# A hybrid decoder block on one core: attention's values behind two mLSTM heads, mLSTM gate rows in one scan, merge gates' tanh in two groups

## The chip, the cores and the metric

The kernel runs on one core of one Trainium2 chip. The metric is the device time of one execution in microseconds (us). Three executions of the kernel before took 822.51, 823.02 and 824.59 us; the median is 823.02 us.

## What is computed

One decoder layer over 512 tokens of width 1024, in float32, with two mixers side by side, a gated merge of them, a ConvFFN and a per-layer embedding. What bears on the change:

```
h = rmsnorm(x); mq, mk, mv, mo, mi, mf, dq, dk, dv, gates = split(h @ w_in)
# branch A, mLSTM, 4 heads x 128: conv4 + SiLU on q and k, and per token and head
#   logf = log_sigmoid(f_pre);  b = cumsum(logf);  m = running maximum of (m + logf, i_pre)
#   weight of key s for query t (s <= t):  exp(b_t - b_s + i_s - m_t)
#   hm = (sum_s weight * (q_t . k_s) * v_s) / max(|sum_s weight * (q_t . k_s)|, exp(-m_t))
ya = (sigmoid(mo) * head_rmsnorm(hm)) @ w_br_m
# branch B, differential attention, 4 heads, queries and keys 2 x 64, values 128
a = softmax(q1 k1 + bias) - lam * softmax(q2 k2 + bias);  hd = a @ dv
yb = (head_rmsnorm(hd) * (1 - lam_init)) @ w_br_d
x = x + (sigmoid(g_a) * ya + sigmoid(g_b) * yb) @ w_out
x = x + ffn(rmsnorm(x));  x = x + ple(...);  out = rmsnorm(x)
```

## The kernel before

Tokens (512) lie along the free axis of most tiles, features on the 128 partitions. A float32 product is made of three single-pass products of split operands (`mm3`, L94): high by high, high by low, low by high, where `split` (L86) casts the high part on ScalarE (L88) and subtracts for the low part on VectorE (L89). `wload` (L100) loads a 512 KB chunk of a weight into one of two `raw` tiles by SyncE's queue and splits it into one of two `whi` and `wlo` tiles. So ScalarE's cast for a projection waits until TensorE has finished with the projection two before it. Such a projection (`proj`) is 24 matmuls of 128x512.

The string `ORDER` (L49) names the steps of the two mixers in the order in which the program records them: `mq0` and `mk0` are projections with convolution and SiLU (`conv_silu`, L215), `if0` the gate rows (`gates`, L314), `ct0` their transposition (L355), `m0` the scores, weights and sums of mLSTM head 0 (`mlstm`, L413), `M0` and `N0` its end and norm, `dv0` the 96 matmuls of the attention's values (`vproj`, L286), `a0` and `A0` an attention head and its norm, `ga0` and `gb0` merge gates (`gate`, L531). What is not in the table (eight of the sixteen merge gates) is made in the merge loop (L580). The framework's scheduler then fixes one order for each engine, by its own estimate of times; weight loads are recorded with a priority ahead of their place. The engines run in that order, each waiting for semaphores at the head of its queue, so a waiting instruction holds up all behind it on that engine.

`gates` makes a 4-row (one per head) log forget gate `lf` and input gate `gi`, and the running maximum `m` by one scan (L341). Then for each of four key blocks j of 128 it scans `lf` again from the block's start (L346), subtracts for the key's column factor (L347), subtracts `m` for the query rows (L348) and writes the rows to `rd` in DRAM (L349). A last row, min(-m, 41), goes there too (L351, L352). `mlstm` loads each block's row as `rb`, broadcast over the partitions (L419), and exponentiates it with the transposed column as bias (L420). `mlstm_end` loads the last row as `em` (L445) and exponentiates it (L446).

In the merge loop a sigmoid is 0.5 + 0.5 tanh(x/2). The tanh of four gates of each pass is recorded behind the last softmax (`issue_after`, L583 to L585). Head 3's norm (`attention_end`, L504) takes a reciprocal root by Ln, Exp and Square (`rsqrt_of`, L152), which need another function table than tanh does.

Of the kernel before, what the change touches and what calls it, by code (L numbers as in the profile page):

```python
# [30 lines left out]
EM_MAX = 41.0  # L31
# [6 lines left out]
C_B = 256  # L38
# [3 lines left out]
ROW_OFF = [0, 512, 896, 1152, 1280]  # L42
# [4 lines left out]


ORDER = """  # L49
if0 mq0 mk0 mq1 mk1 ct0 m0 m1 mk3 mq2 dk0 M0 M1 mk2 bias0 m2 mq3 M2 m3 dq0 dv0 M3 a0 dk1 dq1  # L50
A0 a1 N0 A1 dk2 dq2 N1 ga3 dq3 a2 N2 A2 ga0 ga2 gb1 dk3 N3 a3 gb3 gb2 gb0 ga1 A3
"""


# [1 line left out]
def trunk_kernel(ctx, tc, xT, pT, par, biasT, lamv, w_if, w_in, w_v, w_br, w_out, w_up,  # L56
                 w_down, w_gate, w_ple, gfin, out):
    nc = tc.nc
# [59 lines left out]
    prm = cp.tile([P, NPAR], F32, name="prm")  # L118
# [25 lines left out]
    def sumsq_add(acc, src, first):  # L144
        if first:
            nc.scalar.activation(acc, src, AF.Square)
        else:
            q = tt("hn", "sq")
            nc.scalar.activation(q, src, AF.Square)
            nc.vector.tensor_add(acc, acc, q)  # L150

    def rsqrt_of(r, v, a, before=None, ss=None, n=P):  # L152

        if before is not None:
            with tc.issue_after(before.ins):
                nc.scalar.preload_act_table_set("natural_log_exp_and_others")
        if ss is None:
            nc.scalar.activation(r, v, AF.Ln, scale=2.0 ** -LN_SHIFT)
        else:
            nc.scalar.activation(r, ss, AF.Ln, scale=2.0 ** -LN_SHIFT / n, bias=epsb)  # L160
        nc.scalar.activation(r, r, AF.Exp, scale=-0.5, bias=lnb)
        nc.scalar.activation(a, r, AF.Square)
        nc.vector.scalar_tensor_tensor(a, v, -0.5, a, op0=ALU.mult, op1=ALU.mult)
        nc.vector.scalar_tensor_tensor(r, a, 1.5, r, op0=ALU.add, op1=ALU.mult)

# [17 lines left out]
    h = []  # L183
# [11 lines left out]
    ident = cp.tile([P, P], F32, name="ident")  # L195
# [3 lines left out]
    rB = None  # L199
# [86 lines left out]
    def vproj(i, name, first=None):  # L286
# [24 lines left out]
            vs.append((hi, lo))  # L311
        return vs

    def gates():  # L314

        raw = wp.tile([P, 1024], F32, tag="raw", name="raw", bufs=2)[:, :S]
        w = wp.tile([P, 1024], F32R, tag="whi", name="whi", bufs=2).rearrange("p (k c) -> p k c", c=P)
        with tc.high_priority(offset=180):
            with tc.issue_after(fed.ins):
                nc.sync.dma_start(raw, w_if)  # L320
            split(w[:, :, 0:64], w[:, :, 64:P], raw.rearrange("p (k c) -> p k c", c=64))
        o = ps("mm", "if")
        for k in range(KD):
            for b in range(2):
                nc.tensor.matmul(o, lhsT=w[:, k, :], rhs=h[k][b], start=k + b == 0, stop=k + b == KD)
        gt, g2 = tt("ev", "gt"), tt("hn", "g2")
        nc.vector.tensor_mul(gt[0:36, :], o[0:36, :], rB[0:36, :])
        nc.vector.tensor_mul(g2[0:36, :], o[64:100, :], rB[64:100, :])
        nc.vector.scalar_tensor_tensor(g2[0:36, :], gt[0:36, :], prm[0:36, C_B:C_B + 1], g2[0:36, :],
                                       op0=ALU.add, op1=ALU.add)  # L330
        gi, gf = g2[0:H, :], g2[32:32 + H, :]
        e = tt("rb", "ge")[32:32 + H, :]
        nc.scalar.activation(e, gf, AF.Abs)
        nc.scalar.activation(e, e, AF.Exp, scale=-1.0)
        nc.scalar.activation(e, e, AF.Ln, bias=1.0)
        lf = tt("e", "lf")[0:H, :]
        nc.vector.scalar_tensor_tensor(lf, gf, 0.0, e, op0=ALU.min, op1=ALU.subtract)
        zero = tt("e", "zero")[0:H, :]
        nc.gpsimd.memset(zero, 0.0)
        m = tt("e", "m")[0:H, :]  # L340
        nc.vector.tensor_tensor_scan(m, lf, gi, 0.0, op0=ALU.add, op1=ALU.max)  # L341
        rd = dp.tile([H, NROW], F32, name="rd")
        cols = tt("e", "cols")[0:H, :]
        for j in range(NB):
            r = tt("rb", "rows", S - j * P)[0:H, :]
            nc.vector.tensor_tensor_scan(r, lf[:, j * P:], zero[:, j * P:], 0.0, op0=ALU.add, op1=ALU.add)  # L346
            nc.vector.tensor_sub(cols[:, j * P:(j + 1) * P], gi[:, j * P:(j + 1) * P], r[:, 0:P])  # L347
            nc.vector.tensor_sub(r, r, m[:, j * P:])  # L348
            nc.sync.dma_start(rd[:, ROW_OFF[j]:ROW_OFF[j + 1]], r)  # L349
        r = tt("rb", "rows")[0:H, :]  # L350
        nc.vector.tensor_scalar(r, m, -1.0, EM_MAX, op0=ALU.mult, op1=ALU.min)  # L351
        nc.sync.dma_start(rd[:, ROW_OFF[4]:], r)  # L352
        return rd, cols

    def turn_cols(cols):  # L355
        o = ps("sc", "colp")
        for j in range(NB):
            nc.tensor.transpose(o[:, 4 * j:4 * j + 4], cols[:, j * P:(j + 1) * P], ident[0:H, 0:H])
# [110 lines left out]
    last_softmax = None  # L469
# [61 lines left out]
    def gate(c, name):  # L531
        o = ps("mm", name)
        proj(o, win(c), 0, h)
        t = tt("x", name)
        nc.vector.tensor_mul(t, o, rB)
        return t


    mv = vproj(0, "mv", make_r)
    mq, mk, dq, dk, mo, sums, hm, hd, ga, gb = ({} for _ in range(10))  # L540
    for step in ORDER.split():
        what, i = step[:-1], int(step[-1])
        if what == "if":
            rd, cols = gates()
        elif what == "ct":
            ct = turn_cols(cols)
        elif what == "mq":
            mq[i] = conv_silu(i, 0.5, f"mq{i}")
        elif what == "mk":
            mk[i] = conv_silu(4 + i, 0.5 * P ** -0.5, f"mk{i}")  # L550
        elif what == "mo":
            mo[i] = out_gate(i)
        elif what == "m":
            sums[i] = mlstm(i)
        elif what == "M":
            hm[i] = mlstm_end(i, *sums[i], mo.get(i))
        elif what == "N":
            hm[i] = mlstm_norm(i, *hm[i])
        elif what == "dv":
            dv = vproj(1, "dv")  # L560
        elif what == "bias":
            bias, nlam = make_bias(), make_nlam()
        elif what == "dq":
            dq[i] = queries(8 + i, f"dq{i}")
        elif what == "dk":
            dk[i] = keys(12 + i, f"dk{i}")
# [13 lines left out]
    for m in range(0, KD, 2):  # L580
        js = (m, m + 1)
        gates = [(ga[j] if j in ga else gate(20 + j, "ga"), gb[j] if j in gb else gate(28 + j, "gb")) for j in js]
        with tc.issue_after(last_softmax.ins):  # L583
            for t in (t for pr in gates for t in pr):
                nc.scalar.activation(t, t, AF.Tanh, scale=0.5)  # L585
        outs = []
        for n, (tag, ys) in enumerate((("acc" if m == 2 else "mm", hm), ("mm", hd))):
            w = wload(w_br[m + n])
            outs.append([ps(tag, ("ya", "yb")[n]) for _ in js])
            for i in range(2):  # L590
                proj(outs[n][i], w, 4 * i, ys)
# [21 lines left out]
    rB = rms(acc, "rffn")  # L613
# [17 lines left out]
    for c in range(KF):  # L631
        gt = up(2 * c, "ug", "e")
# [14 lines left out]
    for k in range(2):  # L647
        t = tt("hn", "pt")
# [23 lines left out]
    for j in range(KD):  # L672
        o = ps("mm", "wd")
# [163 lines left out]
def _pack(x, p, rel_bias, norm_mix_g, w_in, b_if, m_conv_w, m_conv_b, m_norm_g, da_lambda, da_norm_g,  # L837
# [2 lines left out]
    w = w_in[0]  # L840
    mq, mk, mv, mo = (w[:, 512 * i:512 * (i + 1)] for i in range(4))
    gif = np.zeros((D, 64), np.float32)
    gif[:, 0:H] = w[:, 2048:2052]
    gif[:, 32:32 + H] = w[:, 2052:2056]
    dq, dk, dv = (w[:, 2056 + 512 * i:2056 + 512 * (i + 1)] for i in range(3))
    win = np.concatenate([mq, mk, dq, dk, mo, w[:, 3592:]], axis=1)
    wv = np.concatenate([v.reshape(4, 2, P, S).transpose(0, 2, 1, 3).reshape(4, P, 2 * S) for v in (mv, dv)])
# [9 lines left out]
    par[:, C_MCONV:C_MCONV + 40] = mc.reshape(5, 8, P).transpose(2, 1, 0).reshape(P, 40)  # L857
    fc = np.concatenate([ffn_conv_w[0], ffn_conv_b], axis=0)
    par[:, C_FCONV:C_FCONV + 176] = fc.reshape(4, 2 * nf, P)[:, order].transpose(2, 1, 0).reshape(P, 176)
    par[0:H, C_B] = b_if[0, :H]  # L860
    par[32:32 + H, C_B] = b_if[0, H:]
    return {
        "xT": _fmajor(x[0]), "pT": _fmajor(p[0, 0]), "par": par, "biasT": _bias_tiles(rel_bias),
        "lamv": da_lambda[0],
# [24 lines left out]
```

## Time and profile before

| | |
|---|---|
| profiled execution | 824.7 us, of which the span of the program's instructions is 822.8 us |
| TensorE (PE) | 809.1 us busy, 98% of the span, 3637 matmuls |
| VectorE (DVE) | 540.6 us, 66% |
| ScalarE (ACT) | 403.0 us, 49% |
| GpSimd (POOL) | 26.3 us, 3% |
| chain of work that ended last | PE 87%, DVE 5%, ACT 4%, DMA 2% |

In rows of the trace, L96 to L98 are the three matmuls of `mm3`, and a tile's name stands before `<-`, what it is made from behind it. `s` are mLSTM scores, `num` its numerator, `hm0ss` and `hd0ss` the sums of squares of head 0 of the two mixers, `ya` and `yb` the two branches' projections in the merge. A matmul's duration is its passage through the array, longer than the distance from one start to the next; so a stall is read from the starts and from the idle time in brackets. The mixers end at about 285 us; the merge's output projection, the ConvFFN and the embedding follow.

### The profile page before, as it was taken

Reading aid. Unit: us, or ns where it says so; the run is one execution under the profiler, and the core shown is the slowest. Engines: PE = TensorE matmul, PEld = TensorE weight load, DVE = VectorE, ACT = ScalarE, POOL = GpSimd, SP = SyncE. Lnnn points to the kernel's source line nnn. Section 1 sums busy time; section 2 is a strip of 40 time slices with the busy share of each in tenths; the row PEclk is TensorE's granted clock in tenths of the full one; section 3 lists DMA queues with packets and bytes.
Section 4 is the critical chain, followed back from the end, with each engine's and each line's share of the span. In section 5 each row is a group of like instructions: output and inputs, shape, how many; then the busy total and the mean of one; then the engine's idle time right before and its main releaser. Section 6 shows DMA issues by size and latency. Waiting matters only on the chain.

```text
span 822.8 us, 9761 instructions
## 1 busy us (share of the span) xinstructions
PE 809.1 (98%) x3637; PEld 661.1 (80%) x3637; DVE 540.6 (66%) x830; ACT 403.0 (49%) x618; POOL 26.3 (3%) x111
## 2 busy tenths in 40 slices
PE   9999999999999999999999999999999999999996
PEld 7777787877877788888888888888888888888885
DVE  7688996589987745455777777777777333343545
ACT  7647855487767533243654444444444432232434
POOL 0001300000000000000000000000000000000000
PEclk9999999999999999999999999999999999999998
DMA  7253351312222232443323322333223333333402
GB/s 249 78 171 101 108 160 59 102 52 77 78 78 76 77 103 84 146 154 103 103 102 103 102 91 89 102 107 123 85 95 103 96 90 96 96 93 106 141 26 102
DMA packets 28262, 84.53 MB, mean 103 GB/s; under 512 B 3332, under 2 KB 5264, under 8 KB 28216
## 3 DMA queue, kind: packets, MB, share of 16 engines
q1 hardware_dynamic: 27400, 81.96, 31.2%
q0 software_dynamic: 528, 1.70, 0.6%
q8 instruction: 28, 0.46, 0.2%
q10 hardware_dynamic: 288, 0.27, 0.1%
q14 instruction: 18, 0.15, 0.1%
HBM read 81.79 MB, written 2.13 MB: 102 GB/s over the span
## 4 chain that ended last, share of the span: by engine, by line
PE 87%; DVE 5%; ACT 4%; DMA 2%; issue 2%; POOL 0%; POOLq 0%; DVEq 0%; SPq 0%; ACTq 0%
PE wd L96 5%; PE uv L97 5%; PE wd L97 5%; PE uv L98 5%; PE uv L96 5%; PE wd L98 5%; PE ug L97 5%; PE ug L98 5%; PE ug L96 5%; PE ga L97 2%; PE ga L96 2%; PE gb L97 2%; PE gb L98 2%; PE ga L98 2%; PE gb L96 2%
## 5 line engine op out<-in xcount | busy, mean ns | idle before, releaser
L88 ACT CAST whi<-raw 128x1024 fp32r<-128x1024 f32 (+1 forms) x136 | 137.6, 1014 | 216.0 <-issue 71.2
L89 DVE TENSOR_TENSOR wlo<-raw,whi 128x1024 fp32r<-128x1024 f32 (+2 forms) x135 | 159.2, 1181 | 90.8 <-ACT whi L88 87.9
L96 PE MATMUL wd<-gh,whi 128*128 128x512 f32 x176 | 68.5, 389 | 0.0
L97 PE MATMUL wd<-gl,whi 128*128 128x512 f32 x176 | 68.5, 389 | 0.0
L98 PE MATMUL wd<-gh,wlo 128*128 128x512 f32 x176 | 68.5, 389 | 0.0
L626 DVE SCALAR_TENSOR_TENSOR y<-u,prm,y 128x512 f32<-128x512 f32 x88 | 65.7, 749 | 1.5
L88 ACT CAST gh<-y 128x512 fp32r<-128x512 f32 x22 | 13.7, 621 | 55.6 <-DVE y L635 55.6
L621 DVE TENSOR_TENSOR u<-uv,rffn 128x512 f32<-128x512 f32 x22 | 15.2, 692 | 38.2 <-PE uv L98 38.2
L98 PEld LDWEIGHTS wd<-gh,wlo 128*128 128x128 f32 x176 | 33.0, 188 | 6.9
L96 PEld LDWEIGHTS wd<-gh,whi 128*128 128x128 f32 x176 | 33.0, 188 | 6.9
L97 PEld LDWEIGHTS wd<-gl,whi 128*128 128x128 f32 x176 | 33.0, 188 | 6.8
L624 ACT ACTIVATE y<-u,prm 128x512 f32<-128x512 f32 x44 | 35.7, 815 | 0.2
L633 ACT ACTIVATE y<-y 128x512 f32<-128x512 f32 x22 | 13.9, 632 | 38.9 <-DVE y L626 38.9
L96 PE MATMUL wo<-mxh,whi 128*128 128x512 f32 x64 | 24.9, 389 | 0.0
L97 PE MATMUL wo<-mxl,whi 128*128 128x512 f32 x64 | 24.9, 389 | 0.0
L98 PE MATMUL wo<-mxh,wlo 128*128 128x512 f32 x64 | 24.9, 389 | 0.0
L89 DVE TENSOR_TENSOR gl<-y,gh 128x512 fp32r<-128x512 f32 x22 | 15.2, 692 | 14.7 <-ACT gh L88 14.7
L489 ACT ACTIVATE e<-e,mx 128x128 f32<-128x128 f32 (+3 forms) x32 | 17.8, 555 | 6.3 <-DVE mx L486 6.0
L226 DVE SCALAR_TENSOR_TENSOR y<-u,prm,y 128x512 f32<-128x512 f32 x24 | 18.0, 749 | 0.0
L486 DVE CUSTOM_DVE_ANT_0 e<-ds,bias 128x128 f32<-128x128 f32 (+3 forms) x32 | 15.4, 483 | 3.2 <-PE ds L482 2.9
L609 DVE TENSOR_TENSOR x<-x,wo 128x512 f32<-128x512 f32 x8 | 5.5, 688 | 17.2 <-PE wo L98 17.2
L678 DVE TENSOR_TENSOR x<-x,wd 128x512 f32<-128x512 f32 x8 | 5.5, 688 | 16.0 <-PE wd L98 16.0
(1089 smaller groups left out, 2202.3 us busy)
## 6 DMA issues: line engine op xcount, KB each, us to landing
raw<-in_w_up SPq DMA_DIRECT2D x44, 512.0 KB, 3.3
raw<-in_w_in SPq DMA_DIRECT2D x36, 512.0 KB, 3.3
raw<-in_w_down SPq DMA_DIRECT2D x16, 512.0 KB, 3.5
x<-in_xT SPq DMA_DIRECT2D x16, 256.0 KB, 4.6
raw<-in_w_br SPq DMA_DIRECT2D x8, 512.0 KB, 3.3
raw<-in_w_out SPq DMA_DIRECT2D x8, 512.0 KB, 3.2
raw<-in_w_gate SPq DMA_DIRECT2D x8, 512.0 KB, 4.5
raw<-in_w_down SPq DMA_DIRECT2D x8, 384.0 KB, 3.1
```

Source lines behind the costliest of these rows:

```text
L88: nc.scalar.copy(hi, src)
L89: nc.vector.tensor_sub(lo, src, f(hi))
L96: nc.tensor.matmul(o, lhsT=lh, rhs=rh, start=start, stop=False)
L97: nc.tensor.matmul(o, lhsT=lh, rhs=rl, start=False, stop=False)
L98: nc.tensor.matmul(o, lhsT=ll, rhs=rh, start=False, stop=stop)
L226: nc.vector.scalar_tensor_tensor(y, u[:, i:i + S], col(c0 + i), y, op0=ALU.mult, op1=ALU.add)
L486: nc.vector.tensor_tensor_reduce(out=e, in0=s[:, :n], in1=bias[hh][:, S - n:], scale=-1.0, scalar=3.0e38, op0=ALU.add, op1=ALU.min, accum_ ...
L489: last_softmax = nc.scalar.activation(e, e, AF.Exp, scale=-1.0, bias=mx[:, z:z + 1], accum_out=mx[:, 2 + z:3 + z])
L621: nc.vector.tensor_mul(u[:, 2:514], o, rB)
L624: nc.scalar.activation(y, u[:, 2:514], AF.Identity, scale=col(c0 + 2), bias=col(c0 + 3))
L626: nc.vector.scalar_tensor_tensor(y, u[:, i:i + S], col(c0 + i), y, op0=ALU.mult, op1=ALU.add)
L633: nc.scalar.activation(gt, gt, AF.Gelu_apprx_tanh)
```

## The change

Three edits, and the pads of the packed weights that go with the second.

1. In `ORDER`, `dv0` moves from behind `dq0`, between `m3` and `M3`, to behind `M1`; the merge gates are taken in another order, so that `ga0`, `ga1`, `gb0`, `gb1` (first pass of the merge) come before `gb3`, `gb2`, `ga3`, `ga2`. A new step `T0` stands behind `a3`.
2. `gates` works on 16 rows, one for each pair of key block j and head, as the gate weights are packed four times over. One scan with a row `keep`, which is 0 where a row's block begins and 1 elsewhere, gives all four cumulated rows; one subtraction gives the columns and one the rows. The last row is written first.
3. `T0` takes the tanh of the gates made so far behind the last softmax; the other gates' tanh is recorded behind the last Square of head 3's root.

```
-if0 mq0 mk0 mq1 mk1 ct0 m0 m1 mk3 mq2 dk0 M0 M1 mk2 bias0 m2 mq3 M2 m3 dq0 dv0 M3 a0 dk1 dq1
+if0 mq0 mk0 mq1 mk1 ct0 m0 m1 mk3 mq2 dk0 M0 M1 dv0 mk2 bias0 m2 mq3 M2 m3 dq0 M3 a0 dk1 dq1
...
+    last_root = None
...
-        nc.scalar.activation(a, r, AF.Square)
+        nonlocal last_root
+        last_root = nc.scalar.activation(a, r, AF.Square)
...
+    HB = H * NB
+    keep = tt("e", "keep")[0:HB, :]
+    nc.gpsimd.memset(keep, 1.0)
+    begin = keep[:, ::P]
+    nc.gpsimd.affine_select(out=begin, in_=begin, pattern=[[-H, NB]], compare_op=ALU.is_ge, fill=0.0, base=-H,
+                            channel_multiplier=1)
+    nc.gpsimd.affine_select(out=begin, in_=begin, pattern=[[-H, NB]], compare_op=ALU.is_ge, fill=1.0, base=0,
+                            channel_multiplier=1)
...
-        cols = tt("e", "cols")[0:H, :]
+        r, cols = tt("rb", "rows")[0:HB, :], tt("e", "cols")[0:HB, :]
+        nc.vector.tensor_tensor_scan(r, keep, lf, 0.0, op0=ALU.mult, op1=ALU.add)
+        nc.vector.tensor_sub(cols, gi, r)
+        nc.vector.tensor_sub(r, r, m)
         for j in range(NB):
-            r = tt("rb", "rows", S - j * P)[0:H, :]
-            nc.vector.tensor_tensor_scan(r, lf[:, j * P:], zero[:, j * P:], 0.0, op0=ALU.add, op1=ALU.add)
-            nc.vector.tensor_sub(cols[:, j * P:(j + 1) * P], gi[:, j * P:(j + 1) * P], r[:, 0:P])
-            nc.vector.tensor_sub(r, r, m[:, j * P:])
-            nc.sync.dma_start(rd[:, ROW_OFF[j]:ROW_OFF[j + 1]], r)
+            nc.sync.dma_start(rd[:, ROW_OFF[j]:ROW_OFF[j + 1]], r[j * H:(j + 1) * H, j * P:])
...
+    def gate_tanh(ts, behind):
+        with tc.issue_after(behind.ins):
+            for t in ts:
+                nc.scalar.activation(t, t, AF.Tanh, scale=0.5)
...
+        elif what == "T":
+            turned_on = [*ga.values(), *gb.values()]
+            gate_tanh(turned_on, last_softmax)
...
-        with tc.issue_after(last_softmax.ins):
-            for t in (t for pr in gates for t in pr):
-                nc.scalar.activation(t, t, AF.Tanh, scale=0.5)
+        gate_tanh([t for pr in gates for t in pr if not any(t is u for u in turned_on)], last_root)
```

First place, ScalarE, from the function table for the first SiLU to the cast `mk0h` of head 0's keys. `u<-y` are the SiLUs' tanh (first `mq0`, then `mk0`), `whi<-raw` casts of weight chunks. Before:

```order
L228 ACT_TABLE_LOAD
L228 ACTIVATE u<-y 128x512
L88 CAST whi<-raw 128x1024
L91 ACTIVATE mq0h<-y 128x512
L224 ACTIVATE y<-u,prm 128x512
L88 CAST whi<-raw 128x1024
L446 ACTIVATE em<-em 128x512
L420 ACTIVATE rb<-rb,ct 128x512
L228 ACTIVATE u<-y 128x512
L420 ACTIVATE rb<-rb,ct 128x384
L420 ACTIVATE rb<-rb,ct 128x256
L91 ACTIVATE mk0h<-y 128x512
```

Now, from the first SiLU's tanh on:

```order
L231 ACTIVATE u<-y 128x512
L459 ACTIVATE em<-em 128x512
L88 CAST whi<-raw 128x1024
L91 ACTIVATE mq0h<-y 128x512
L227 ACTIVATE y<-u,prm 128x512
L459 ACTIVATE em<-em 128x512
L88 CAST whi<-raw 128x1024
L231 ACTIVATE u<-y 128x512
L433 ACTIVATE rb<-rb,ct 128x512
L433 ACTIVATE rb<-rb,ct 128x384
L433 ACTIVATE rb<-rb,ct 128x256
L91 ACTIVATE mk0h<-y 128x512
```

Two `em` stand there now, the second ahead of a weight cast that before stood ahead of the one `em`; the second SiLU's tanh has gone ahead of all `rb`.

Second place, SyncE's DMA queue, from the last short row written to `rd` on. Before:

```order
L352 DMA rd<-rows 4x512
L419 DMA rb<-rd 128x512
L419 DMA rb<-rd 128x384
L419 DMA rb<-rd 128x256
L419 DMA rbs<-rd 128x128 x2
L445 DMA em<-rd 128x512
L105 DMA raw<-in_w_in 128x1024
L445 DMA em<-rd 128x512 x3
```

Now:

```order
L361 DMA rd<-rows 4x128
L458 DMA em<-rd 128x512
L105 DMA raw<-in_w_in 128x1024
L432 DMA rb<-rd 128x512
L432 DMA rb<-rd 128x384
L432 DMA rb<-rd 128x256
L432 DMA rbs<-rd 128x128 x2
L458 DMA em<-rd 128x512
L105 DMA raw<-in_w_in 128x1024
L458 DMA em<-rd 128x512 x2
```

One `em` and a weight chunk now stand ahead of the five broadcast rows of head 0, and the second `em` behind them. (Before, that weight chunk stood among the writes of `rd`.)

Third place, ScalarE again, at head 3's norm in the merge; `v` and `y` are the square and the scaled copy of attention's output, `r` its Ln and Exp. Before:

```order
L513 ACTIVATE v<-av_2437 128x512
L519 ACTIVATE y<-av_2437,prm 128x512
L156 ACT_TABLE_LOAD
L585 ACT_TABLE_LOAD
L585 ACTIVATE ga<-ga 128x512
L88 CAST whi<-raw 128x1024
L160 ACT_TABLE_LOAD
L160 ACTIVATE r<-hd3ss,lnb 128x512
L161 ACT_TABLE_LOAD
L161 ACTIVATE r<-r,lnb 128x512
L162 ACTIVATE hd3ss<-r 128x512
```

Now:

```order
L526 ACTIVATE v<-av_2429 128x512
L532 ACTIVATE y<-av_2429,prm 128x512
L158 ACT_TABLE_LOAD
L88 CAST whi<-raw 128x1024
L162 ACTIVATE r<-hd3ss,lnb 128x512
L163 ACTIVATE r<-r,lnb 128x512
L165 ACTIVATE hd3ss<-r 128x512
L554 ACT_TABLE_LOAD
```

One tanh and three loads of function tables between the square and the root's end are gone; a load of the tanh's table stands behind it.

## Rows read from the trace of the kernel before

**Rows 1.** Windows: busy time of each engine (instructions), granted clock, DMA share, GB/s.
```profile
63.50:66.50 3.00, 3.00 (x9) 2.38 (x8) 3.00 (x6) 2.02 (x4) 0.25 (x1) 0.51 0.01 4
110.00:120.00 10.00, 10.00 (x51) 8.16 (x49) 9.67 (x19) 5.63 (x11) 0.35 (x2) 1.00 0.33 89
140.00:150.00 10.00, 10.00 (x46) 8.29 (x45) 2.45 (x2) 2.11 (x2) 0.00 (x0) 1.00 0.34 105
270.00:280.00 10.00, 9.15 (x40) 7.24 (x39) 5.29 (x9) 4.84 (x6) 0.00 (x0) 1.00 0.17 54
```
**Rows 2.** Waits of PE: who waited for whom, us in total, times, longest.
```profile
PE s L96 <- ACT mk0h L91: 2.4, 1, 2.4
...
PE yb L96 <- DVE hdh L526: 0.9, 1, 0.9
...
PE hm0ss L170 <- ACT csph L168: 0.4, 1, 0.4
...
PE hd0ss L170 <- ACT csph L168: 0.2, 1, 0.2
```
**Rows 3.** Timeline of PE, 59 to 64 us: start, duration, what, idle before.
```profile
59.14 0.39 PE L97 MATMUL mk<-h5l,whi 128*128 128x512 f32 x1
59.37 0.39 PE L98 MATMUL mk<-h5h,wlo 128*128 128x512 f32 x1
62.15 0.50 PE L96 MATMUL s<-mq0h,mk0h 128*128 128x512 f32 x1 [2.39 <-ACT mk0h L91]
...
63.56 0.63 PE L96 MATMUL mk<-h6h,whi 128*128 128x512 f32 x1
63.99 0.63 PE L97 MATMUL mk<-h6l,whi 128*128 128x512 f32 x1
```
**Rows 4.** Timeline of ACT, 55 to 62 us.
```profile
55.20 1.03 ACT L88 CAST whi<-raw 128x1024 fp32r<-128x1024 f32 x1
58.91 0.63 ACT L446 ACTIVATE em<-em 128x512 f32<-128x512 f32 x1 [2.68 <-DMA em<-rd]
...
60.59 1.00 ACT L420 ACTIVATE rb<-rb,ct 128x384 f32<-128x384 f32 x2
61.49 0.61 ACT L91 ACTIVATE mk0h<-y 128x512 fp32r<-128x512 f32 x1
```
**Rows 5.** Timeline of SyncE's queue, 51 to 55 us: start and length of issue.
```profile
51.72 1.29 SPq L419 DMA_DIRECT2D rb<-rd  x3
...
54.00 0.43 SPq L445 DMA_DIRECT2D em<-rd  x1
```
**Rows 6.** DMA issues, 45 to 63 us: KB each, us from issue to landing.
```profile
em<-rd SPq DMA_DIRECT2D x4, 256.0 KB, 5.4
rb<-rd SPq DMA_DIRECT2D x1, 256.0 KB, 3.3
```
**Rows 7.** Groups of DVE, 41 to 51 us: count, busy us, mean ns, idle before.
```profile
L346 DVE TENSOR_TENSOR_SCAN rows<-lf,zero 4x512 f32<-4x512 f32 (+3 forms) x4 | 3.1, 796 | 0.0
...
L348 DVE TENSOR_TENSOR rows<-rows,m 4x512 f32<-4x512 f32 (+3 forms) x4 | 1.8, 472 | 0.0
...
L347 DVE TENSOR_TENSOR cols<-g,rows 4x128 f32<-4x128 f32 x4 | 1.0, 267 | 0.0
```
**Rows 8.** Timeline of DVE, 41 to 61 us.
```profile
41.17 1.20 DVE L341 TENSOR_TENSOR_SCAN m<-lf,g 4x512 f32<-4x512 f32 x1
...
51.02 0.67 DVE L221 TENSOR_TENSOR u<-mk,rmix 128x512 f32<-128x512 f32 x1
...
58.55 1.22 DVE L89 TENSOR_TENSOR wlo<-raw,whi 128x1024 fp32r<-128x1024 f32 x1
60.71 0.69 DVE L229 SCALAR_TENSOR_TENSOR y<-u,y 128x512 f32<-128x512 f32 x1 [0.94 <-ACT u L228]
```
**Rows 9.** Timeline of ACT, 267 to 274 us.
```profile
267.39 1.28 ACT L585 ACT_TABLE_LOAD   x1
...
272.28 1.28 ACT L161 ACT_TABLE_LOAD   x1
```

More of the change, by code (lines that the diff above doesn't have):

```diff
@@ L49 @@
 ORDER = """
-if0 mq0 mk0 mq1 mk1 ct0 m0 m1 mk3 mq2 dk0 M0 M1 mk2 bias0 m2 mq3 M2 m3 dq0 dv0 M3 a0 dk1 dq1
-A0 a1 N0 A1 dk2 dq2 N1 ga3 dq3 a2 N2 A2 ga0 ga2 gb1 dk3 N3 a3 gb3 gb2 gb0 ga1 A3
+if0 mq0 mk0 mq1 mk1 ct0 m0 m1 mk3 mq2 dk0 M0 M1 dv0 mk2 bias0 m2 mq3 M2 m3 dq0 M3 a0 dk1 dq1
+A0 a1 N0 A1 dk2 dq2 N1 ga0 dq3 a2 N2 A2 ga1 gb0 gb1 dk3 N3 a3 T0 gb3 gb2 ga3 ga2 A3
 """
@@ L326, in gates @@
         gt, g2 = tt("ev", "gt"), tt("hn", "g2")
-        nc.vector.tensor_mul(gt[0:36, :], o[0:36, :], rB[0:36, :])
-        nc.vector.tensor_mul(g2[0:36, :], o[64:100, :], rB[64:100, :])
-        nc.vector.scalar_tensor_tensor(g2[0:36, :], gt[0:36, :], prm[0:36, C_B:C_B + 1], g2[0:36, :],
+        n = 32 + HB
+        nc.vector.tensor_mul(gt[0:n, :], o[0:n, :], rB[0:n, :])
+        nc.vector.tensor_mul(g2[0:n, :], o[64:64 + n, :], rB[64:64 + n, :])
+        nc.vector.scalar_tensor_tensor(g2[0:n, :], gt[0:n, :], prm[0:n, C_B:C_B + 1], g2[0:n, :],
                                        op0=ALU.add, op1=ALU.add)
-        gi, gf = g2[0:H, :], g2[32:32 + H, :]
-        e = tt("rb", "ge")[32:32 + H, :]
+        gi, gf = g2[0:HB, :], g2[32:n, :]
+        e = tt("rb", "ge")[32:n, :]
         nc.scalar.activation(e, gf, AF.Abs)
@@ L335, in gates @@
         nc.scalar.activation(e, e, AF.Ln, bias=1.0)
-        lf = tt("e", "lf")[0:H, :]
+        lf = tt("e", "lf")[0:HB, :]
         nc.vector.scalar_tensor_tensor(lf, gf, 0.0, e, op0=ALU.min, op1=ALU.subtract)
-        zero = tt("e", "zero")[0:H, :]
-        nc.gpsimd.memset(zero, 0.0)
-        m = tt("e", "m")[0:H, :]
+        m = tt("e", "m")[0:HB, :]
         nc.vector.tensor_tensor_scan(m, lf, gi, 0.0, op0=ALU.add, op1=ALU.max)
         rd = dp.tile([H, NROW], F32, name="rd")
-        cols = tt("e", "cols")[0:H, :]
+        r, cols = tt("rb", "rows")[0:HB, :], tt("e", "cols")[0:HB, :]
+        nc.vector.tensor_tensor_scan(r, keep, lf, 0.0, op0=ALU.mult, op1=ALU.add)
+        nc.vector.tensor_sub(cols, gi, r)
+        nc.vector.tensor_sub(r, r, m)
         for j in range(NB):
-            r = tt("rb", "rows", S - j * P)[0:H, :]
-            nc.vector.tensor_tensor_scan(r, lf[:, j * P:], zero[:, j * P:], 0.0, op0=ALU.add, op1=ALU.add)
-            nc.vector.tensor_sub(cols[:, j * P:(j + 1) * P], gi[:, j * P:(j + 1) * P], r[:, 0:P])
-            nc.vector.tensor_sub(r, r, m[:, j * P:])
-            nc.sync.dma_start(rd[:, ROW_OFF[j]:ROW_OFF[j + 1]], r)
+            nc.sync.dma_start(rd[:, ROW_OFF[j]:ROW_OFF[j + 1]], r[j * H:(j + 1) * H, j * P:])
         r = tt("rb", "rows")[0:H, :]
-        nc.vector.tensor_scalar(r, m, -1.0, EM_MAX, op0=ALU.mult, op1=ALU.min)
+        nc.vector.tensor_scalar(r, m[0:H], -1.0, EM_MAX, op0=ALU.mult, op1=ALU.min)
         nc.sync.dma_start(rd[:, ROW_OFF[4]:], r)
@@ L357, in turn_cols @@
         for j in range(NB):
-            nc.tensor.transpose(o[:, 4 * j:4 * j + 4], cols[:, j * P:(j + 1) * P], ident[0:H, 0:H])
+            nc.tensor.transpose(o[:, HB * j:HB * (j + 1)], cols[:, j * P:(j + 1) * P], ident[0:HB, 0:HB])
         ct = cp.tile([P, NB * H], F32, name="ct")
-        nc.vector.tensor_copy(ct, o[:, :NB * H])
+        nc.vector.tensor_copy(ct.rearrange("p (j h) -> p j h", h=H),
+                              o[:, :NB * (HB + H)].rearrange("p (j c) -> p j c", c=HB + H)[:, :, 0:H])
         return ct
@@ L842, in _pack @@
     gif = np.zeros((D, 64), np.float32)
-    gif[:, 0:H] = w[:, 2048:2052]
-    gif[:, 32:32 + H] = w[:, 2052:2056]
+    for j in range(NB):
+        gif[:, j * H:(j + 1) * H] = w[:, 2048:2052]
+        gif[:, 32 + j * H:32 + (j + 1) * H] = w[:, 2052:2056]
     dq, dk, dv = (w[:, 2056 + 512 * i:2056 + 512 * (i + 1)] for i in range(3))
@@ L859, in _pack @@
     par[:, C_FCONV:C_FCONV + 176] = fc.reshape(4, 2 * nf, P)[:, order].transpose(2, 1, 0).reshape(P, 176)
-    par[0:H, C_B] = b_if[0, :H]
-    par[32:32 + H, C_B] = b_if[0, H:]
+    par[0:NB * H, C_B] = np.tile(b_if[0, :H], NB)
+    par[32:32 + NB * H, C_B] = np.tile(b_if[0, H:], NB)
     return {
```

## The prediction

> **What bounds the kernel now.** I read the page first: TensorE (PE) is busy for 809.1 of 822.8 us, and 87% of the chain that ended last is PE. The change adds and removes no matmul of size, so it can win only what PE loses by waiting or by its clock. The windows come next: in most stretches of 10 us PE is busy for all 10 at clock 1.00, as at 140 us [rows 1]. PE's waits show where it is not: 2.4 us once before the scores `s` of mLSTM head 0, 0.9 before `yb` in the merge, 0.4 and 0.2 before two sums of squares [rows 2]. The timeline of PE gives the first its whole price. Matmuls of 512 columns start 0.23 us apart; after the start at 59.37 the next could come at 59.60 and comes at 62.15, so 2.55 us are lost. A little later starts lie 0.43 apart (63.56 and 63.99) [rows 3]: the granted clock is 0.51 from 63.5 to 66.5 us [rows 1], the lower of its two levels (1.2 and 2.4 GHz), after PE had sat idle for 2.39 us. Half speed over 3.0 us costs 1.5 us more. These places, some 5.6 us together, are the stock from which the change can draw; VectorE (DVE), at 9.67 of 10 us from 110 us on [rows 1], makes PE wait nowhere there.
>
> Who makes PE wait at 59.60? ScalarE (ACT) shows it: it sat idle for 2.68 us until `em` had landed, and behind `em` in its queue stood `rb`, the SiLU's tanh, two more `rb` and then `mk0h`, for which the scores wait [rows 4].
>
> **Part 1, the gate rows.** Twelve DVE instructions go: four scans, four column and four row subtractions, 3.1 + 1.0 + 1.8 = 5.9 us busy [rows 7]. One scan, for which I take the 1.20 us of `m` at the same 512 elements (4 or 16 partitions should not matter: a full-width subtraction takes 0.67 to 0.69 us, [rows 8]), and two subtractions of 0.68 come: 2.6 us. DVE gains 3.3 us here. But `u` of `mk0` (0.67, [rows 8]) now stands ahead of the last tap of `mq0`, and starts overlap by some 0.1, so `mq0`'s SiLU comes about 2.3 us sooner. DVE is no bound here; its gain reaches PE only through the DMA and ACT queues, and there the order changes too.
>
> SyncE's queue: scan from 42.30 (41.17 and 1.13 to the next start), then last row, columns, one tap and rows end near 45.7. Four short writes at 0.35 us bring the first `em`'s issue to about 47.2. A weight chunk follows near 48.2, behind DVE's split of the chunk two before it. Then five broadcasts at 0.43 us an issue (the first three took 1.29, [rows 5]), and the second `em` at about 51.0, 3.0 us before the one `em` of before.
>
> Its landing decides, because ACT now has the second `em` ahead of a weight cast, the tanh, three `rb` and `mk0h`. A broadcast with nothing before it takes 3.3 us from issue, one in a train 5.4 [rows 6]. Before, six broadcasts in a row were issued from 51.72 [rows 5]; the last landed when ACT's idle time ended, at 58.91 [rows 4]. So each after the first added (58.91 - 51.72 - 3.3) / 5 = 0.78 us. Now the second `em` is the eighth of a train from 47.2: 47.2 + 3.3 + 7 x 0.78 = 56.0 us. Lower bound: no delay by the train, 51.0 + 3.3 = 54.3. Upper bound: no earlier than before, 58.9. I take 56.0, because the train is the same kind of transfers.
>
> The Trainium skill ("DMA: Bandwidth & Descriptors", "Queues, rings and completion order") says that each DMA engine consumes the descriptors of a queue's ring in their order. That speaks against the lower bound, since all of these leave SyncE's queue; by it the eighth waits for the seven before it, and 5.4 against 3.3 us in the rows agrees. With the lower bound the sum below would be 0.6 us better.
>
> From the landing L: `em` 0.63, cast 1.03, tanh 0.61 (as `mk0h`), three `rb` 1.6 (two took 1.00), `mk0h` 0.61 [rows 4], less overlaps of 0.08: L + 4.2. DVE's side gives the same: split of the weight chunk 1.22 and the last SiLU step 0.69 [rows 8] behind the cast. So the scores start at 56.0 + 4.2 = 60.2. The scheduler has left PE two matmuls fewer ahead of them (16 of `mk3`, not 18), so PE is there at 59.14 and loses 1.06 us: 1.5 us gained of 2.55. With L at 54.3 the cast still waits for PE's release of the buffer, as before at 55.20 [rows 4], and the scores start no sooner than 59.65: 2.1 gained. With L at 58.9: 1.4 lost. The two meet, nothing gained, at L = 57.5.
>
> The clock: a wait of 0.9 us (that of `yb`) left it at 1.00 from 270 to 280 us, one of 2.39 lowered it [rows 1, 2]. 1.06 us lies nearer the first, so I count the 1.5 us as gained; bounds 0 and 1.5.
>
> **Part 2, the values behind `M1`.** PE does the same 96 matmuls, 96 x 0.23 = 22 us, earlier. Before, they filled the time in which DVE had little to do (2.45 of 10 us at 140) [rows 1]; now they stand where DVE was full and lets it drain. What they covered lies bare: the third head's scores now have `mk2`'s SiLU, a chain of some 7 us, under `mq3` (24 x 0.23 = 5.5) and seven matmuls of `mo` (1.6), and the cast `mk2h` has a weight cast ahead of it that waits for the end of `mq3`: 5.65 + 1.03 + 0.61 = 7.3 against 7.1. I charge 0.3 us for such places. Bounds: -0.5 (nothing late, and the fuller DVE of before was worth something) and 2.4, as at the first scores. Head 0's end stands in ACT's queue ahead of the next head's `rb` now, and attention head 0's square ahead of two casts behind it; the 0.4 and 0.2 us waits of the sums of squares are then partly gone, but fewer matmuls lie ahead of them. I take half, 0.3 gained; bounds 0 and 0.6.
>
> **Part 3, tanh in two groups.** Before, between head 3's square and its root ACT loads a function table, loads tanh's, does one tanh, loads again, and again between Ln and Exp: 1.28 us a load [rows 9]. Three loads and a tanh, 4.4 us, leave that stretch. PE cannot gain 4.4: it waited 0.9 there [rows 2], because 37 matmuls lay between the second half of `hd3ss` and `yb`. Now 27 lie there, 6.1 us. The chain under them: `ya`'s last four matmuls release the buffer (1.1), cast 1.03, Ln, Exp and Square 2.1, three DVE steps 2.1: 6.3 to 6.5. So 0.1 to 0.3 us of wait remains of 0.9 with its restart: 0.7 gained, bounds -0.3 and 0.9. The second group's tanh comes behind the root, under `yb`, and costs nothing: the second pass needs it only after 24 more matmuls.
>
> **The sum.** 1.5 + 1.5 + 0.3 + 0.7 - 0.3 = 3.7 us. From the profiled execution, 824.7 us (span 822.8 and 1.9 around it): 821.0. The runs' median, 823.0, lies 1.7 below the profiled one; so 819.3 as a median.
>
> **The rivals.**
> (a) The wait changes its name only. The second `em` lands near 57.5, PE loses its 2.5 us and the clock falls as before; the merge and the sums remain, 0.7: 822.3. For it: the first `em` and a 512 KB chunk are added ahead. Against it: an issue 3.0 us earlier.
> (b) The stall shrinks and the clock falls all the same, 1.5 us: 820.8. For it: between 0.9 and 2.39 us no row shows what happens. The Trainium skill ("TensorE: Matmul & The Clock Gate", "What's actually happening") says that the monitor behind the clock runs freely and does not start anew with the kernel; so where a gap falls would matter as well as its length, and the row at 270 us excuses one gap only. No run here shows a gap of about 1 us elsewhere.
> (c) Slower: the second `em` lands later than the one of before. Place: ACT's queue at 53 us; behind it stand the cast of `mq2`'s weights, the tanh and `mk0h`. At L = 59.5 the scores start 1.5 us later than before and two matmuls behind (2.0 lost in all), and a longer gap buys a second stretch at half clock (1.5): 3.5 lost, 0.7 gained, 825.8. From L = 58.2 on the whole is slower than before even without that second stretch, and that needs 7.2 us from issue where before the median was 5.4 [rows 6].
>
> **How the numbers follow.** Chances: forecast 0.55, (a) 0.18, (b) 0.12, (c) 0.08, anything else 0.07. This kernel's time tells 0.3% (2.5 us) from no change: faster is below 820.5. The forecast's own range is 817.3 (lower bounds of the DMA and of part 2, 0.9 at the merge) to 821.2 (0.8 more for part 2, half of the clock's gain); nine tenths of it are faster, and half of (b): 0.5 + 0.06, and a little of the rest, 0.58. (a), half of (b) and the forecast's end are within: 0.31. (c) and half of the rest are slower: 0.11. The range for 8 in 10 runs from 817.0 to 823.5; it takes in (a) and (b) and leaves out (c).
>
> **What would show it.** Right: PE's wait before `s` near 1 us with ACT's second `em` idle until about 56; clock 1.00 from 60 to 70 us; the wait before `yb` under 0.3; two table loads fewer from the last softmax on; no PE wait over 0.5 us between 115 and 160. Wrong: a second `em` after 57.5, a clock under 1 anywhere between 55 and 170 us, or a new wait before the third head's scores or the first attention head's.

## The result, and the profile after

The kernel after takes 818.87 us (median of 8 executions, 818.38 to 821.35), the kernel before 822.69 us (8 executions, 821.88 to 826.15). The ratio is 0.9948, with a 95% interval of 0.9935 to 0.9960: 3.8 us, 0.5%, faster. On another chip the same kernel gave 0.9935 (0.9919 to 0.9952). The profiled execution took 821.35 us, its span 819.2 us.

One thing must be set aside before the two profiles are compared. In this execution of after the first products (`mvp`) still start 0.43 us apart until 10.9 us; in a second profile of the same kernel (`after_again` below), whose span is 816.1 us, they do so only until about 7 us. So the first gate-row matmul comes at 31.72 us here, at 29.00 there, and at 29.43 in the profile of before. I therefore compare from that matmul to the end: 793.4 us before, 787.5 after, and 787.1 in the second profile of after.

These are TensorE's waits of after, all that the view shows (who waited for whom, us in total, times, longest):

```profile
PE warm L125 <- DVE idle L122: 1.5, 1, 1.5
PE s L96 <- ACT mk0h L91: 1.4, 1, 1.4
PE mvp L96 <- DVE whi L283: 0.8, 1, 0.8
```

The first and third belong to the kernel's first microseconds. Of the waits of before [rows 2] only that of the first scores is left, 1.4 instead of 2.4 us; `yb`, `hm0ss` and `hd0ss` wait no more. One more is absent here that the prediction had not priced. This is its line in the list of before, and below it that in the second profile of after, where half of it is left:

```profile
PE num L96 <- ACT pph L88: 0.4, 1, 0.4
PE num L96 <- ACT pph L88: 0.2, 1, 0.2
```

Windows of after, to be held against [rows 1] (from:to, length, busy us of PE, PEld, DVE, ACT, POOL with instructions, granted clock, DMA share, GB/s):

```profile
65.80:68.80 3.00, 3.00 (x18) 2.56 (x17) 3.00 (x5) 2.52 (x4) 0.00 (x0) 1.00 0.00 0
60.00:70.00 10.00, 8.61 (x42) 6.92 (x41) 8.78 (x13) 8.50 (x17) 1.98 (x6) 1.00 0.27 83
110.00:120.00 10.00, 10.00 (x46) 8.26 (x44) 3.88 (x5) 4.03 (x5) 0.00 (x0) 1.00 0.30 106
140.00:150.00 10.00, 10.00 (x48) 8.01 (x47) 9.07 (x15) 9.21 (x16) 0.87 (x3) 1.00 0.22 73
270.00:280.00 10.00, 10.00 (x45) 7.93 (x44) 9.01 (x13) 6.57 (x9) 0.00 (x0) 1.00 0.32 107
```

The clock behind the first scores is 1.00, where 0.51 stood. VectorE's load has changed places: 3.88 of 10 us at 110 us, where the attention's values now are, and 9.07 at 140 us. TensorE is busy throughout in both. From 270 to 280 us it is busy 0.85 us longer than before.

The first scores, TensorE and ScalarE of after (start, duration, what, idle before):

```profile
61.26 0.39 PE L96 MATMUL mk<-h5h,whi 128*128 128x512 f32 x1
63.03 0.50 PE L96 MATMUL s<-mq0h,mk0h 128*128 128x512 f32 x1 [1.39 <-ACT mk0h L91]
63.37 0.39 PE L97 MATMUL s<-mq0l,mk0h 128*128 128x512 f32 x1
```
```profile
54.95 0.80 ACT L227 ACTIVATE y<-u,prm 128x512 f32<-128x512 f32 x1
58.84 0.63 ACT L459 ACTIVATE em<-em 128x512 f32<-128x512 f32 x1 [3.10 <-DMA em<-rd]
59.38 1.03 ACT L88 CAST whi<-raw 128x1024 fp32r<-128x1024 f32 x1
60.32 0.63 ACT L231 ACTIVATE u<-y 128x512 f32<-128x512 f32 x1
60.85 1.61 ACT L433 ACTIVATE rb<-rb,ct 128x512 f32<-128x512 f32 x3
62.37 0.61 ACT L91 ACTIVATE mk0h<-y 128x512 fp32r<-128x512 f32 x1
```

ScalarE sits idle for 3.10 us until the second `em` has landed at 58.84, and the scores start 4.19 us later, as forecast (L + 4.2). TensorE could have gone on at 61.49 and loses 1.54 us. SyncE's queue ahead of it, and VectorE's gate rows (new groups, 41 to 51 us):

```profile
49.30 0.35 SPq L458 DMA_DIRECT2D em<-rd  x1
50.39 0.36 SPq L105 DMA_DIRECT2D raw<-in_w_in  x1
50.84 1.32 SPq L432 DMA_DIRECT2D rb<-rd  x3
52.21 0.90 SPq L432 DMA_DIRECT2D rbs<-rd  x2
53.16 0.43 SPq L458 DMA_DIRECT2D em<-rd  x1
```
```profile
L357 DVE TENSOR_TENSOR_SCAN rows<-keep,lf 16x512 f32<-16x512 f32 x1 | 1.2, 1186 | 0.0
...
L359 DVE TENSOR_TENSOR rows<-rows,m 16x512 f32<-16x512 f32 x1 | 0.7, 674 | 0.0
L358 DVE TENSOR_TENSOR cols<-g,rows 16x512 f32<-16x512 f32 x1 | 0.7, 673 | 0.0
```

One scan and two subtractions, 2.53 us, stand for the twelve instructions of [rows 7]. From the first `em`'s issue to the second's landing it takes 9.54 us; the forecast had 8.76.

ScalarE in the merge, after:

```profile
264.30 0.68 ACT L532 ACTIVATE y<-av,prm 128x512 f32<-128x512 f32 x1
265.00 1.28 ACT L158 ACT_TABLE_LOAD   x1
266.89 1.05 ACT L88 CAST whi<-raw 128x1024 fp32r<-128x1024 f32 x1 [0.61 <-PE ya L97]
267.85 0.68 ACT L162 ACTIVATE r<-hd3ss,lnb 128x512 f32<-128x512 f32 x1
268.56 0.72 ACT L163 ACTIVATE r<-r,lnb 128x512 f32<-128x512 f32 x1
269.31 0.60 ACT L165 ACTIVATE hd3ss<-r 128x512 f32<-128x512 f32 x1
269.94 1.28 ACT L554 ACT_TABLE_LOAD   x1
```

The loads of [rows 9], between square and root's end, are gone: one load is left there (265.00), and one follows behind (269.94).

### The profile page after: what moved, and what is told of

It is laid out like the page before. It is cut to its first block, busy times and chain, and to the rows that moved or that the text cites. A ratio compares the mean times of both kernels' runs of the same rounds, so it can differ in the third digit from the quotient of the medians.

```text
span 819.2 us, 9753 instructions
## 1 busy us (share of the span) xinstructions
PE 808.1 (99%) x3637; PEld 662.4 (81%) x3637; DVE 537.4 (66%) x821; ACT 400.1 (49%) x616; POOL 27.8 (3%) x113
## 4 chain that ended last, share of the span: by engine, by line
PE 92%; DVE 3%; ACT 2%; issue 1%; DMA 1%; POOL 0%; SPq 0%; POOLq 0%; DVEq 0%; ACTq 0%
PE uv L97 5%; PE wd L96 5%; PE wd L98 5%; PE uv L96 5%; PE uv L98 5%; PE wd L97 5%; PE ug L97 5%; PE ug L96 5%; PE ug L98 5%; PE gb L96 2%; PE ga L98 2%; PE ga L97 2%; PE gb L98 2%; PE ga L96 2%; PE gb L97 2%; PE wo L96 2%
## 5 line engine op out<-in xcount | busy, mean ns | idle before, releaser
L639 POOL MEMSET u<- 128x2 f32 x44 | 4.3, 99 | 359.3 <-DVE y L645 347.9
```

## The experiments

Ratios are to the kernel before on the same chip, with 95% intervals. "Wait" is TensorE's wait before the first scores in the profile.

**Each part alone.** Three kernels are the kernel before with one part of the change: the gate rows, the move of `dv0` in `ORDER`, and the tanh in two groups with the gates in their new order.

```
rows_only:  gates() on 16 rows, weights packed four times; ORDER as before
dv_only:   -... M0 M1 mk2 bias0 m2 mq3 M2 m3 dq0 dv0 M3 ...
           +... M0 M1 dv0 mk2 bias0 m2 mq3 M2 m3 dq0 M3 ...
tanh_only:  T0 and last_root; gates as ga0 ga1 gb0 gb1 gb3 gb2 ga3 ga2
```

> The kernel before with part 1 alone (gate rows of 16 pairs in one scan). Theory: the first scores' wait falls from 2.4 to about 1.4 us and no stretch at half clock follows, so the gain is 1.0 + 1.5 = 2.5 us: ratio about 0.997, clock 1.00 from 60 to 70 us; the waits of hm0ss, hd0ss and yb stay at 0.4, 0.2 and 0.9. Rival A (the half clock behind the first scores belongs to the one profiled execution of before): ratio about 0.999. Rival B (the whole gain of 3.8 us comes from here, the other parts give nothing): ratio 0.9954.

> The kernel before with part 2 alone (the attention's values behind the second mLSTM head's end). Theory: the waits before hm0ss and hd0ss (0.4 and 0.2 us, about 0.8 with their restart) go and no new wait comes before the third head's scores: ratio 0.999, wait of s in all 2.4 us. Rival A (the third head's scores come late, as the prediction charged, by 0.3 to 2.4 us): a second wait before s, ratio 1.000 to 1.002. Rival B (the move is where the change gains most): ratio below 0.997.

> The kernel before with part 3 alone (tanh of the merge gates in two groups, gates in the new order). Theory: the wait before yb (0.9 us) goes, with its restart about 1.0 us: ratio 0.9988; two table loads fewer; everything ahead of the third attention head as before. Rival (the stretch is bound by the release of the weight buffer and the cast, not by the tables): yb's wait stays at 0.6 us or more, ratio 1.000.

| kernel | ratio | wait, us | clock, 60 to 70 us |
|---|---|---|---|
| rows_only | 0.9964 (0.9951 to 0.9978) | 1.0 | 1.00 |
| dv_only | 0.9980 (0.9967 to 0.9993) | 2.8 | 0.66 |
| tanh_only | 0.9988 (0.9978 to 0.9999) | 2.0 | 0.83 |

The gate rows are the largest part, as their theory said. Rival B's ratio, 0.9954, lies inside the interval, so the time doesn't exclude it; the waits do, for `yb` and `hd0ss` still wait:

```profile
PE s L96 <- ACT mk0h L91: 1.0, 1, 1.0
PE yb L96 <- DVE hdh L536: 0.8, 1, 0.8
...
PE hd0ss L170 <- ACT csph L168: 0.2, 1, 0.2
```

`hm0ss`, which was expected to wait as before, does not. In tanh_only `yb` no longer waits, as its theory said. Its first scores show a half clock behind a wait of 1.96 us (matmuls of 512 columns take 0.43 us to the next start from 62.35 to 65.45 us):

```profile
62.00 0.55 PE L96 MATMUL s<-mq0h,mk0h 128*128 128x512 f32 x1 [1.96 <-ACT mk0h L91]
```

The move alone brought a surprise. In its profile `hm0ss` still waits (0.3), `hd0ss` does not, no wait has come before the third head's scores, and `yb` no longer waits either, though the code of the tanh is that of before:

```profile
268.28 0.69 ACT L519 ACTIVATE y<-av,prm 128x512 f32<-128x512 f32 x1
268.99 1.28 ACT L156 ACT_TABLE_LOAD   x1
270.28 1.05 ACT L88 CAST whi<-raw 128x1024 fp32r<-128x1024 f32 x1
271.24 0.68 ACT L160 ACTIVATE r<-hd3ss,lnb 128x512 f32<-128x512 f32 x1
```

The framework's scheduler has put the tanh behind the root by itself. So the wait before `yb` is saved by part 2 as well as by part 3, and their gains can't be added. The ratios don't resolve this: 0.36 + 0.20 + 0.12 = 0.68%, against 0.52% for all three (0.65% on the other chip), each with an interval of 0.1 or more to either side.

**Undoing one part.** The kernel after without part 3, and without part 2.

```
tanh_back:  after, with the tanh behind the last softmax and the gates in the old order
dv_back:    after, with ORDER "... m2 mq3 M2 m3 dq0 dv0 M3 ..."
```

> The kernel after without part 3 (all tanh of the merge gates behind the last softmax again, gates in the old order). Theory A (part 3 is what took the wait before yb away): yb waits 0.6 to 0.9 us again, 819.7, ratio to the kernel after 1.001. Theory B (with the values moved, the scheduler puts the tanh behind head 3's root by itself, as in the kernel with part 2 alone, where no wait before yb was left): no wait before yb, one table load between the square and the root, 818.9.

> The kernel after with the values back at their old place, between dq0 and M3 (parts 1 and 3 alone). Theory (the parts add by place): the waits of hm0ss and hd0ss are back at 0.3 and 0.2 us, that of yb is gone by part 3: 0.6 to 1.2 us slower than the kernel after, 819.8, ratio to the kernel before 0.995. Rival (the move costs what the prediction charged for the third head's scores, 0.3 us or more): 818.6 or less, ratio 0.993.

> The kernel after once more, beside the others of this call: 818.9 us, the wait before s at 1.4 us or 0.3 us to either side of it, clock 1.00 behind it.

| kernel | median, us | ratio | wait, us |
|---|---|---|---|
| after_again | 819.02 (818.29 to 820.12) | 0.9935 (0.9919 to 0.9952) | 0.7 |
| tanh_back | 818.95 (818.57 to 819.80) | 0.9933 (0.9916 to 0.9949) | 1.2 |
| dv_back | 819.48 (819.23 to 819.68) | 0.9955 (0.9942 to 0.9968) | 1.2 |

Without part 3 nothing is lost: theory B. There is one table load between square and root and no wait before `yb`. Part 3 does its work only where part 2 is missing. Without part 2 the time is 0.5 us above after's (on another chip, so this is weak); `hd0ss` waits again (0.2), `yb` doesn't, and `hm0ss`, expected to wait again, doesn't either. The rival, that the move costs something, has nothing for it.

**What the first scores wait for.** Theory: the second `em`, by its place in ScalarE's queue. Its Exp is recorded behind another instruction that needs no `em`, in the kernel after (run on two chips) and in the kernel before.

```
-        nc.scalar.activation(em, em, AF.Exp)
         ad = tt("hn", "ad")
-        nc.scalar.activation(ad, den, AF.Abs)
+        behind = nc.scalar.activation(ad, den, AF.Abs)
+        with tc.issue_after(behind.ins):
+            nc.scalar.activation(em, em, AF.Exp)
```

> The kernel after, with the Exp of em recorded behind the Abs of den, so that no em stands in ScalarE's queue ahead of mk0h; its loads are where they were. Theory: the second em's landing sets the 1.4 us that are left before the first scores, so the wait falls to 0.4 us or less and the time by about 1 us, to 817.9. Rival A (the weight cast, which waits until TensorE has released its buffer, or the tanh behind it, is late anyway): the wait stays at 1.2 us or more, 818.9. Rival B (given back: the Exp, 0.63 us, now lies between Abs and the head's norm, and hm0ss waits for it): s's wait is gone and a wait of about 0.6 us before hm0ss comes, 818.5.

> The kernel after with em's Exp behind the Abs of den, on the same chip as the kernel after. Theory (em's landing was the last thing the first scores waited for, 1.4 us): 1.0 to 1.4 us less than the kernel after, 817.6. Rival (the 0.5 us between the earlier medians is between the chips): no difference.

> The kernel before with nothing of the change but em's Exp recorded behind the Abs of den; the four scans and their subtractions stay. Theory (em's place in ScalarE's queue makes the stall, the gate rows' length on VectorE does not): the first scores wait for the two short rbs instead, which land near 51.7 + 3.3 + 4 x 0.78 = 58.1 us, so mk0h starts near 58.6 and the wait falls from 2.4 to 0.8 us or less, with no stretch at half clock: ratio 0.996 to 0.997, as much as the kernel with part 1 alone (0.9964). Rival (the rows have to be ready sooner, as part 1 makes them): the wait stays at 1.5 us or more, ratio 0.998 to 1.000.

In the kernel after the wait is gone: 817.89 us (817.52 to 818.16, ratio 0.9930) and 818.28 us (817.60 to 818.73, ratio 0.9921; after_again beside it 819.02). The second gain, 0.7 us, is less than the 1.0 to 1.4 expected, but after_again loses only 0.88 us before the scores. In em_late_again the scores follow the last `mk` matmul directly; VectorE's column copy, not a landing, now precedes the tanh:

```profile
59.72 0.39 PE L96 MATMUL mk<-h5h,whi 128*128 128x512 f32 x1
59.95 0.42 PE L96 MATMUL s<-mq0h,mk0h 128*128 128x512 f32 x1
```
```profile
57.14 0.63 ACT L231 ACTIVATE u<-y 128x512 f32<-128x512 f32 x1 [0.42 <-DVE ct L372]
```

Nothing is given back at `hm0ss` (rival B). This version beats both kernels, by 0.7 to 1.0 us over after; the ten executions of the one and the fourteen of the other overlap a little (818.3 to 818.7), so the size is less certain than the lost wait.

In the kernel before, the same edit gives less than I expected: ratio 0.9992 (0.9983 to 1.0001).

```profile
PE s L96 <- ACT mk0h L91: 1.5, 1, 1.5
PE yb L96 <- DVE hdh L527: 0.8, 1, 0.8
PE hm0ss L170 <- ACT csph L168: 0.6, 1, 0.6
PE den L170 <- ACT csph L168: 0.3, 1, 0.3
```
```profile
57.99 1.23 ACT L420 ACTIVATE rb<-rb,ct 128x512 f32<-128x512 f32 x2 [1.73 <-DVE ct L360]
```

The wait falls by 0.9 us and stays at 1.5, because the first `rb` waits for the transposed columns `ct` and the two short `rbs` have come ahead of `mk0h`; the waits before `hm0ss` and `den` are 0.2 and 0.3 us longer than in before. So the rival is borne out: the rows have to be ready sooner, and part 1 makes them so. Here only both edits together remove the stall.

**The price of a pause for the clock.** Three kernels are the kernel after with ten pauses of TensorE in the up projections, from about 412 us on; they add work and change no result. The edit of the first is shown; the other two make the copies shorter.

```
+    def pause(n):
+        with tc.issue_after(last_mm.ins):
+            nc.tensor.matmul(o, lhsT=ones, rhs=h2[0][0], start=True, stop=True)
+        nc.scalar.copy(t, o)                   # and n - 1 copies of t
+        resume = nc.tensor.matmul(..., rhs=t)  # the projections follow behind it
```

> The kernel after with ten pauses of TensorE in the ConvFFN's up projections, 22 us apart: a matmul, one to five copies of 128x512 on ScalarE (some 0.55 us each) that wait for it, a matmul that waits for them, in the order 2, 4, 1, 3, 5, 3, 1, 4, 2, 5 copies; so pauses of about 0.9, 1.5, 2.0, 2.6 and 3.1 us, each twice. Theory (length decides): the pauses up to 1.5 us leave the granted clock at 1.00, as the 1.4 us before the first scores did; those of 2.6 and 3.1 are followed by a stretch of some 3 us at half clock (1.5 us lost each). Rival (the place in time decides as well): two pauses of the same length differ, one with a stretch at half clock and one without.

> The kernel after with ten pauses of TensorE as before, of one copy of 128x512 and a second of 0, 128, 256, 384 or 512 columns, in the order 0, 2, 1, 3, 4, 2, 3, 1, 4, 0 (times 128): pauses between 1.2 and 2.4 us, each twice. Theory (length decides, and the 1.4 us before the first scores are on the safe side, 2.0 us in the kernel with part 3 alone were not): the two of 1.2 keep the clock, the two of 2.4 lose 1.5 us each, and the change lies between 1.4 and 2.0 us. Rival (the place decides as well): two pauses of one length differ.

> The kernel after with ten pauses of TensorE as before, each of one copy of 640, 768, 896 or 1024 columns, in the order 5, 7, 6, 8, 7, 5, 8, 6, 7, 8 (times 128): pauses of about 1.3 to 1.7 us. Theory: pauses as long as those left before the first scores (0.7 to 1.4 us) lower the clock at no place, and those of 1.5 to 1.7 don't either, since at 2.1 it came one time in two: clock 1.00 behind all ten. Rival (the 1.4 us were lucky): at least one of the ten is followed by a stretch at half clock.

Copies took longer than I had put for the first kernel, so its pauses were 1.21 to 4.76 us; the others had 1.21 to 2.42 us and 1.31 to 1.63 us. What followed, over all thirty:

| pause, us | pauses | followed by a stretch of starts 0.43 us apart | starts in it |
|---|---|---|---|
| 1.21 to 1.63 | 14 | 0 | |
| 2.10 to 2.43 | 10 | 5 | 7 or 8 |
| 3.08 to 4.37 | 5 | 5 | 6 or 7 |
| 4.76 | 1 | 1 | 13 |

Two pauses of one length in pauses_short, and the 10 us around each:

```profile
439.39 0.50 PE L663 MATMUL pd<-csph,ones 128*128 128x512 f32 x1 [2.21 <-ACT csph L662]
540.13 0.50 PE L663 MATMUL pd<-csph,ones 128*128 128x512 f32 x1 [2.21 <-ACT csph L662]
```
```profile
437.00:447.00 10.00, 7.79 (x34) 6.30 (x34) 6.22 (x8) 4.73 (x7) 0.10 (x1) 1.00 0.16 53
537.50:547.50 10.00, 7.79 (x27) 5.94 (x26) 4.80 (x6) 3.15 (x5) 0.10 (x1) 0.83 0.17 54
```

The same 2.21 us left the granted clock at 1.00 once and brought it to 0.83 over 10 us, 27 matmuls instead of 34, the other time. Below 1.7 us none of the fourteen did, as at the longest here:

```profile
485.57 0.39 PE L664 MATMUL pd<-csph 128*128 128x512 bf16 x1 [1.63 <-ACT csph L663]
```
```profile
483.00:493.00 10.00, 8.37 (x38) 6.58 (x37) 6.12 (x8) 5.00 (x6) 0.10 (x1) 1.00 0.17 57
```

So both were partly right. In these thirty, all pauses up to 1.63 us and all from 3.08 us on went one way, and from 2.1 to 2.4 us something besides the length decided; in tanh_only 1.96 us had sufficed. Two outcomes at one length fit with what the Trainium skill says ("TensorE: Matmul & The Clock Gate", "What's actually happening"), that the monitor runs freely and does not start anew with the kernel. That the place in time is what decides is not shown, since no run varies it alone.

## Why the prediction was right, and where its sizes were off

The forecast of 819.3 us and the measured 818.87 differ by 0.4 us; the sum of 3.7 us stands against 3.8 between the medians. Part of this closeness is luck: on the chip of after_again the medians differ by 5.45 us (824.47 and 819.02). The steps, one by one:

**The first scores (1.5 forecast).** The mechanism is shown: the second `em`'s landing sets their start, and with its Exp out of the way the wait is gone. TensorE loses 1.54 us in the profile of after, so 1.0 was gained there. The other four kernels with this order waited 0.72, 0.97, 1.16 and 1.19 us; a wait costs some 0.16 us more than its length (1.54 for 1.39), so the five lose 1.2 us on average where I had 1.06. The landing varies by 0.7 us between these executions: 8.87 us from the first `em`'s issue in after_again, 9.54 in after. Rivals (a) and (c), a landing at 57.5 or later, are excluded for all of them: even after's 58.84 is 56.6 once the late start (2.29 us) is taken off.

**The clock (1.5 forecast).** Gained in the profile: 1.00 where 0.51 stood. Rival (b), that a wait near 1 us lowers the clock all the same, has nothing for it in any profile: the fourteen short pauses didn't lower it, nor did the waits of 0.7 to 1.5 us before the first scores in the six profiles that had them. (One of rows_only's six executions, without a profile, had a mean clock of 0.996 and took 822.57 us, the others 820.84 at most; its cause is open.)

But the size was read from one execution. The 2.39 us of before lie where the clock falls only sometimes, and the list of before's executions shows it: of the 52 timed with the experiments 19 had a mean granted clock of 0.996 or less, the others 0.997 or more; of the 34 executions of after, em_late, em_late_again, after_again, tanh_back and dv_back none fell under 0.997. The mean tells the stretch: among the profiles of kernels without pauses, the three that show it (before, dv_only, tanh_only) have 0.994 or 0.995, the others 0.997 or more. The 19 took 824.4 us in the median and the other 33 822.9, so the price of 1.5 us was right where it was paid. On average the term was worth nearer 1.5 x 19 / 52 = 0.5 than 1.5 us; what a median shows of it depends on how many such executions it has.

**The sums of squares (0.3 forecast).** Too small. Starts in before are late by 0.56 us at `hm0ss` and 0.40 at `hd0ss`, 1.0 together, and the forecast allowed 0.6 at most; in after both are under 0.15. `hm0ss` is part 1's: it is late by 0.26 to 0.75 us in the four kernels without that part and on time in all with it. `hd0ss` is part 2's: late by 0.4 us in every kernel without the move and on time in all with it. One `num` that I had left out is late by 0.61 us in before and on time in the profile of after, but by 0.32 in after_again and 0.4 in em_late and em_late_again, so that gain is not sure.

**The merge (0.7 forecast).** The start of `yb` was late by 1.02 us and is now on time, so 1.0, more than the bound of 0.9. The chain under it has the forecast length, 6.3 us from `hd3ss` at 265.77 to the end of `hdh` at 272.10; but the 28 starts of TensorE from there to `yb` take 6.4 us, so no wait is left where I had counted 6.1 and kept 0.1 to 0.3:

```profile
265.77 0.39 PE L531 MATMUL hd3ss<-cspl,ones 128*128 128x512 f32 x1
272.15 0.72 PE L96 MATMUL yb<-hdh,whi 128*128 128x512 f32 x2
```
```profile
271.41 0.69 DVE L539 SCALAR_TENSOR_TENSOR hdh<-y,r 128x512 fp32r<-128x512 f32 x1
```

What I had wrong is the cause: I charged it to part 3, and part 2 does it too, since the scheduler then orders the tanh as part 3 would. The prediction read the order of the whole change and never asked which edit made it.

**The move of the values (-0.3 forecast).** No charge: between 85 and 260 us no start of after is late by more than 0.13 us. VectorE's load moved as described and TensorE waited nowhere.

**The sum.** From the first gate-row matmul on, the two profiles differ by 5.9 us: 1.0 for the first scores, 1.5 for the clock, 1.6 for the sums with `num`, 1.0 for the merge, and some 0.8 that I haven't traced to single places. The median moved by less; the clock's 1.5 us were lost in only some of before's executions. That a sum of 3.7 met 3.8 is in part errors that cancel: the clock term too large, sums and merge too small by 1.0 us together without `num` (1.6 with it), and 0.3 charged for a move that cost nothing.

## What to carry to other kernels

When an engine idles behind a DMA, look at what stands between that load and the instruction that others wait for: moving one exponential of 0.6 us, needed much later, out of the way took the rest of the stall. Then try the edit alone and the change without it, because a scheduler's reordering can make one edit do another's work. And before a clock loss from one profile enters a sum, look at how many executions show it.

## What was not expected of the hardware

A pause of 2.1 to 2.4 us lowered the granted clock 5 times in 10, at equal lengths; up to 1.63 us never in 14, from 3.08 us on always in 6; a wait of 1.96 us in tanh_only did once. The stretch at half clock that follows begins up to 1.3 us after the restart and costs about 1.5 us (7 starts, 0.2 us late each), and after the 4.76 us pause 2.6 us (13 starts).
